# A mixture-of-experts stage with other weight rows, bfloat16 pair maps, and a branch and two down projections at other places

## The chip, the cores and the metric

The program runs on one core of one Trainium2 chip. The metric is device microseconds (us) from start to end of one execution, given as a median of runs. The engines of the core are named as in the profile: PE (TensorE, matrix products), PEld (its weight loads), DVE (VectorE), ACT (ScalarE), POOL (GpSimd) and SP (SyncE, which here only issues the transfers of weights).

## The reference, cut to what matters

Two transformer blocks work on 256 tokens of width 1024, in float32. The first one ends in a hierarchical mixture of experts: 4 groups of 4 experts, each token goes to 2 experts of one group, and each expert is a gated layer of width 512.

```python
def one_group(args):
    wg_g, wu_g, wd_g, comb_g = args
    hid = jax.nn.silu(jnp.einsum('td,edf->tef', t, wg_g)) * jnp.einsum('td,edf->tef', t, wu_g)
    return jnp.einsum('tef,efd->td', hid * comb_g[:, :, None], wd_g)

y = jnp.sum(lax.map(one_group, (wg, wu, wd, jnp.moveaxis(combine, 1, 0))), axis=0)
...
x = x + g2 * hierarchical_moe(hx2, ...)
return rmsnorm(x, final_norm_g)
```

The second block projects the result with `w_in_2` (10240 columns) and goes on with convolution, two kinds of attention and a dense layer of width 4096.

## The kernel before

One function issues everything by hand. Each engine runs its own instructions in the order in which they are written, and waits by semaphores for others. Weights come through one list, `plan`: SP loads the next entry (1 MB, with `kpn` as the layout) into one of 24 slots whenever `pump()` finds a free one, within the limits in `lim`. So loads run ahead of the work in a fixed order: per expert two halves of gate and up, then two halves of down, and after the last expert the pieces of `w_in_2`.

**Routing.** After attention, `xa_T` transposes x for the router's product, DVE ranks the logits, `posm` gets each token's slot (up to 64 tokens, `CAP`, in an expert) and `comb` its weight. `gather` builds the 64 columns of each expert in a group of four (`xg`) by a product with a 0/1 map (L1113).

**One expert e** (16 in a loop) is
- `moe_up(e, k0, k1)`, L1186: gate and up products side by side, two matmuls of 64 slots by 512 for each of eight slices of 128 rows; the trace counts each one twice,
- `moe_act(e)`, L1197 on ACT (silu) and L1198 on DVE (times up), result in `gm`,
- `moe_hT(e)`, L1204: four transposes of that result on PE; L1206 on DVE multiplies them by the slot weights `wb`,
- `moe_down(e)`, L1215: the down product, after which DVE (L1224, L1227) and ACT (L1225) scale it and split it in two parts (`RB`).

**One pair p of experts** has besides
- `weigh(p)`, L1151 and L1153 on DVE: the 0/1 map of tokens to slots, float32, and the map times `comb`,
- `slot_weights()`, L1160: a product with ones that lays the weights out by slot, copied to `wb` by L1161,
- `build_DT(p)`, L1168 and L1170: the map transposed in float32, one full and two half transposes for each half of the tokens, copied by ACT (L1172) to `DT`,
- `moe_comb(p)`, L1233: eight matmuls that add the pair's results into the four banks `yb`.

`weigh` stands at the end of an even expert; `slot_weights`, `build_DT` belong to the odd one behind it. In most experts a quarter or a half of `moe_up(e)` is written ahead of `moe_hT(e - 1)` and `moe_down(e - 1)`. A flag, `early`, turns this off:

```python
early = e >= 13 or (e and e % 4 == 0)
if not early:
    moe_up(e, 0, 2)
if e % 2:
    slot_weights()
if e:
    moe_hT(e - 1)
if not early:
    moe_up(e, 2, 4)
```

**The branch.** `beyond()` handles an expert with more than 64 tokens. Every engine loads the flag `over` (L1308) and branches (L1309); with these inputs the body is jumped over. It stands at the head of the last expert, e = 15, between `moe_comb(6)`, `weigh(7)` and `slot_weights`. The body uses PE, DVE, ACT and POOL.

Of the kernel before, what the change touches and what calls it, by code (L numbers as in the profile page):

```python
# [86 lines left out]
def body(tc, d, out, dbg=None, stop=None):  # L87
# [238 lines left out]
    def ld_x(t):  # L326
        nc.sync.dma_start(t, d["x"].rearrange("(t p) d -> p t d", p=128))
        nc.sync.dma_start(br, bass.AP(tensor=d["br"].tensor, offset=d["br"].offset, ap=[[0, 128], [1, 20]]))
        nc.sync.dma_start(wr, kpn(d["wr"]))

# [58 lines left out]
    for e in range(NE):  # L389
        for kh in range(2):  # L390
            for nm, w in (("g", d["w_gate"]), ("u", d["w_up"])):
                plan.append(((nm, e, kh), [128, 4, 512], kpn(w[e][512 * kh:512 * kh + 512, :])))
        for kh in range(2):
            plan.append((("d", e, kh), [128, 2, 1024], kpn(d["w_down"][e][256 * kh:256 * kh + 256, :])))
    w2 = d["w_in_2"]
# [207 lines left out]
    def mod_cols(Tn):  # L603
        bk = trans_bank([bm[:, Tn, j * 128:(j + 1) * 128] for j in range(4)])
        return bk.rearrange("p (j g r) -> p r g j", j=4, g=4)
# [538 lines left out]
    DT = None  # L1144
    wb = cp.tile([128, 2, 64], F32, name="wb")

    def map_of(i):
        return RA[:, 2, 256 * i:256 * i + 256].rearrange("p (t e c) -> p t e c", t=2, e=2)

    def weigh(p):  # L1150
        V.tensor_tensor(map_of(0), iot.to_broadcast([128, 2, 2, 64]),  # L1151
                        posm[:, :, 2 * p:2 * p + 2, None].to_broadcast([128, 2, 2, 64]), op=OP.is_equal)
        V.tensor_tensor(map_of(1), map_of(0),  # L1153
                        comb[:, :, 2 * p:2 * p + 2, None].to_broadcast([128, 2, 2, 64]), op=OP.mult)

    def slot_weights():

        bk = bank()
        for tt in range(2):
            T.matmul(bk[:, 0:128], ones, map_of(1)[:, tt].rearrange("p e c -> p (e c)"), start=(tt == 0), stop=(tt == 1))  # L1160
        V.tensor_copy(wb.rearrange("p e c -> p (e c)"), bk[:, 0:128])  # L1161

    def build_DT(p):

        bk = bank()
        Dp = map_of(0)
        for tt in range(2):
            T.transpose(bk[:, tt * 128:(tt + 1) * 128], Dp[:, tt].rearrange("p e c -> p (e c)"), ident)  # L1168
            for s in range(2):
                T.matmul(bk[64 * s:64 * s + 64, (2 + tt) * 128:(3 + tt) * 128], Dp[:, tt, 1 - s, :], ident,  # L1170
                         start=True, stop=True, skip_group_check=True)
        A.activation(DT, bk, AF.Copy)  # L1172
# [36 lines left out]
    def moe_down(e):  # L1209
        b = bank()  # L1210
        t = hTm.pop(e)
        for k in range(4):
# [4 lines left out]
            if k % 2:  # L1217
                raw_done(("d", e, k // 2))
        pump()
        pd = [(slice(64 * j, 64 * j + 64), j ^ (e % 2)) for j in range(2)]  # L1220
        if e == NE - 1:
# [85 lines left out]
    def beyond():  # L1307
        flag = nc.values_load(over[0:1, 0:1], min_val=0, max_val=1)  # L1308
        with tc.If(flag > 0):  # L1309
# [5 lines left out]
            h2T = take([128, 8, 256], F32, "h2b")  # L1315
            for k0, bk in transposed_pairs(lambda tt, k: xb[:, tt, k * 128:(k + 1) * 128], 8):
                for kk in range(2):
# [3 lines left out]
            hbT = take([128, 4, 256], F32, "hbT")  # L1321
            tmpD = take([128, 2, 512], F32, "tmpD")
            for e in range(NE):
                wt = {}
                for nm, w in (("g", d["w_gate"]), ("u", d["w_up"])):
                    for kh in range(2):
                        wt[nm, kh] = take([128, 4, 512], F32, "fb")
                        G.dma_start(wt[nm, kh], kpn(w[e][512 * kh:512 * kh + 512, :]))
                for tt in range(2):
# [10 lines left out]
                for dh in range(2):  # L1340
                    G.dma_start(wd[dh], kpn(d["w_down"][e][:, 512 * dh:512 * dh + 512]))
                for k0, bk in transposed_pairs(lambda tt, k: hb[:, tt, k * 128:(k + 1) * 128], 4):
                    V.tensor_copy(hbT[:, k0:k0 + 2], bk)
                for tt in range(2):
                    for dh in range(2):
                        bk = bank()
                        for k in range(4):
                            T.matmul(bk, hbT[:, k, tt * 128:(tt + 1) * 128], wd[dh][:, k, :], start=(k == 0), stop=(k == 3))
                        V.tensor_tensor(tmpD[:, dh], bk, gm[:, dh], op=OP.mult)
                        V.tensor_tensor(yb[tt][dh], yb[tt][dh], tmpD[:, dh], op=OP.add)  # L1350
                give(*wd)
            give(hb, hbT, tmpD, h2T)
        A.preload_act_table_set("silu_and_others")

    for e in range(NE):
        if e == NE - 3:
            lim[:] = [12, 4]
        if e == NE - 1:
            beyond()
        if e == 0:  # L1360
# [18 lines left out]
        if e == 1:  # L1379
# [31 lines left out]
        if e == 12:  # L1411
# [380 lines left out]
```

## Time and profile before

| | us |
|---|---|
| median of 3 runs | 1113.88 (1113.6 to 1114.24) |
| the profiled execution's own time | 1112.18 |
| its span, first to last instruction | 1110.4 |
| PE busy | 1057.2 (95%) |
| DVE busy | 606.0 (55%) |
| ACT busy | 434.3 (39%) |

The profiled execution lies 1.78 us above its span and 1.70 us under the median. The mean granted clock of PE is 0.987 of full speed. Busy shares are means over stages with different limits, so a stage is read from its own rows: in a timeline row the first two numbers are start and length, and brackets give the idle time before it and what ended that. The experts run from 318 to 559.5 us, the second block follows.

### The profile page before, as it was taken

What the parts mean: (1) busy time and instruction counts of PE and PEld (TensorE: products, weight loads), DVE (VectorE), ACT (ScalarE), POOL (GpSimd) and SP (SyncE); (2) the same over time, 40 slices, a digit from 0 to 9 for tenths busy, and PEclk for the clock granted to TensorE, in tenths of its full rate; (3) what the DMA queues carried; (4) which work ended last, traced back from release to release, by engine and by line L of the source; (5) the groups of instructions that cost most, each with busy time, mean ns of one, the idle gap of its engine ahead of it and who ended that gap; (6) DMA issues with size and microseconds to landing.
All of it is one profiled execution on the core that took longest, in us unless ns stands there. A gap on an engine that the chain in (4) does not pass through costs nothing.

```text
span 1110.4 us, 15119 instructions
## 1 busy us (share of the span) xinstructions
PE 1057.2 (95%) x6115; PEld 789.3 (71%) x6115; DVE 606.0 (55%) x930; ACT 434.3 (39%) x744; POOL 93.3 (8%) x99
## 2 busy tenths in 40 slices
PE   5999999899989999998689999999999999999998
PEld 4678876555743434343279878999888889998997
DVE  4554435666534343433175655767455676666544
ACT  4754213556312222222163476444435125343222
POOL 0000303000101010100010444000000000000000
PEclk9999999999989999999899999999999999999999
DMA  9979852454868999999913342534757565545611
GB/s 337 405 259 400 278 181 73 176 190 162 326 230 315 393 395 392 394 395 394 387 61 115 114 153 76 190 124 155 258 184 251 204 207 172 190 154 189 225 41 38
DMA packets 111087, 254.95 MB, mean 230 GB/s; under 512 B 5434, under 2 KB 8475, under 8 KB 108451
## 3 DMA queue, kind: packets, MB, share of 16 engines
q1 hardware_dynamic: 109666, 249.20, 62.4%
q0 software_dynamic: 1344, 4.72, 1.4%
q8 instruction: 50, 0.82, 0.3%
q14 instruction: 27, 0.21, 0.1%
HBM read 249.71 MB, written 4.19 MB: 229 GB/s over the span
## 4 chain that ended last, share of the span: by engine, by line
PE 48%; DMA 1%; DVE 1%; ACT 1%; SPq 0%; issue 0%; DVEq 0%; ACTq 0%
PE acc L223 26%; PE acc L243 11%; PE b L243 7%; DMA raw<-in_w_in 1%; PE b L483 1%; PE b L1499 1%; PE b L1521 1%; PE b L1577 1%; PE b L1601 1%; PE b L1215 0%; PE b L1532 0%; SPq L138 0%; PE b L1520 0%; DVE split L198 0%; ACT junkB L476 0%
## 5 line engine op out<-in xcount | busy, mean ns | idle before, releaser
L198 DVE TENSOR_TENSOR split<-raw,split 128x1024 fp32r<-128x1024 f32 (+2 forms) x226 | 267.5, 1212 | 79.5 <-ACT split L197 77.4
L197 ACT ACTIVATE split<-raw 128x1024 fp32r<-128x1024 f32 (+2 forms) x170 | 168.2, 1035 | 42.4 <-PE acc L223 14.5
L243 PE MATMUL acc<-uh,split 128*128 128x256 f32 x640 | 122.9, 288 | 1.4 <-ACT uh L498 1.4
L1186 PE MATMUL b<-raw,xg 128*64 128x512 f32 x512 | 115.8, 595 | 0.0
L243 PEld LDWEIGHTS acc<-uh,split 128*128 128x128 f32 x640 | 102.7, 193 | 2.5 <-ACT uh L498 1.6
L223 PE MATMUL acc<-split,uh 128*128 128x512 f32 x320 | 101.2, 392 | 0.0
L243 PE MATMUL b<-fh,split 128*128 128x256 f32 x512 | 93.9, 283 | 0.3 <-DVE split L198 0.3
L243 PE MATMUL acc<-ul,split 128*128 128x256 f32 x320 | 91.4, 286 | 0.1
L223 PE MATMUL acc<-split,hidT 128*128 128x512 f32 x384 | 88.4, 389 | 0.0
L223 PEld LDWEIGHTS acc<-split,hidT 128*128 128x128 f32 x384 | 71.6, 188 | 14.6
L243 PEld LDWEIGHTS b<-fh,split 128*128 128x128 f32 x512 | 80.4, 192 | 0.8 <-DVE split L198 0.5
L1186 PEld LDWEIGHTS b<-raw,xg 128*64 128x64 f32 x512 | 36.5, 137 | 61.1 <-issue 59.0
L243 PE MATMUL b<-fl,split 128*128 128x256 f32 x256 | 72.4, 283 | 0.0
L223 PEld LDWEIGHTS acc<-split,uh 128*128 128x128 f32 x320 | 60.1, 188 | 12.8
L1225 ACT ACTIVATE RB<-RA 64x512 fp32r<-64x512 f32 x32 | 20.1, 628 | 121.8 <-DVE RA L1224 120.2
L1215 PE MATMUL b<-raw,RA 128*64 128x512 f32 x256 | 60.0, 611 | 5.3 <-ACT xg L1121 2.5
L243 PEld LDWEIGHTS acc<-ul,split 128*128 128x128 f32 x320 | 61.9, 193 | 0.7 <-DVE ul L499 0.6
L223 PE MATMUL acc<-split,ul 128*128 128x512 f32 x160 | 62.3, 390 | 0.0
L1224 DVE TENSOR_TENSOR RA<-b,gm 64x512 f32<-64x512 f32 x32 | 22.0, 689 | 71.9 <-PE b L1215 71.4
L243 PEld LDWEIGHTS b<-fl,split 128*128 128x128 f32 x256 | 49.1, 192 | 0.3
L1215 PEld LDWEIGHTS b<-raw,RA 128*64 128x64 f32 x256 | 19.0, 141 | 39.8 <-issue 34.4
L223 PE MATMUL acc<-split,memTh 128*128 128x512 f32 x128 | 44.0, 413 | 3.2 <-ACT split L197 1.7
(398 smaller groups left out, 1741.4 us busy)
## 6 DMA issues: line engine op xcount, KB each, us to landing
raw<-in_w_up SPq DMA_DIRECT2D x48, 1024.0 KB, 5.5
raw<-in_w_down SPq DMA_DIRECT2D x48, 1024.0 KB, 9.1
raw<-in_w_in SPq DMA_DIRECT2D x46, 1024.0 KB, 7.9
raw<-in_w_gate SPq DMA_DIRECT2D x32, 1024.0 KB, 14.8
raw<-in_w_mod SPq DMA_DIRECT2D x24, 1024.0 KB, 11.3
raw<-in_w_mem_kv SPq DMA_DIRECT2D x8, 1024.0 KB, 14.1
raw<-in_w_out SPq DMA_DIRECT2D x8, 1024.0 KB, 5.0
raw<-in_w_conv_out SPq DMA_DIRECT2D x4, 1024.0 KB, 4.9
```

Of the source, the lines that this page charges most:

```text
L197: A.activation(s[:, 0], src, AF.Copy)
L198: V.tensor_tensor(s[:, 1], src, s[:, 0].bitcast(F32), op=OP.subtract)
L223: T.matmul(job.accs[m], x(k + kk), s[:, w, kk, :], start=job.start and first and kk == 0 and j == 0, stop=job.stop and last and kk == kg - ...
L243: T.matmul(bk[:, o:o + 256], s[:, w, kk, 128 * b:128 * b + 128], x(k + kk), start=first and b % per == 0 and r == 0 and kk == 0 and j == 0 ...
L483: T.transpose(bk[0:m, i * 128:i * 128 + p], s, ident)
L1186: T.matmul(b[64 * j:64 * j + 64, :], lt, raw((nm, e, k // 4))[:, k % 4, :], start=(k == 0), stop=(k == 7), skip_group_check=True)
L1215: T.matmul(b[64 * j:64 * j + 64, :], t[:, k, :], raw(("d", e, k // 2))[:, k % 2, 512 * dh:512 * dh + 512], start=(k == 0), stop=(k == 3), ...
L1224: V.tensor_tensor(RA[r, dh, :], b[r, :], gm[r, dh], op=OP.mult)
L1225: A.activation(RB[r, 0, dh, :], RA[r, dh, :], AF.Copy)
L1499: T.matmul(zb[i + j][:, o:o + 256 - k0], skT[sl, p, k0:k0 + 128], sqT[sl, p, k0:256], start=(o == 0), stop=False, skip_group_check=True)
L1521: T.matmul(b[:, 0:384], negL, v, start=False, stop=(n == 1), skip_group_check=True)
L1577: T.matmul(b[:, 0:256], xqT[:, 2 * h + dt, tt * 128:(tt + 1) * 128], mkT[:, 2 * h + dt, :], start=(dt == 0), stop=(dt == 1))
```

## The change

**Rows of 8 KB.** For gate, up and down weights (and the router's) a partition now holds neighbouring rows (`runs`), not every 128th one (`kpn`): gate and up come in one run of 8 KB for a partition where there were four of 2 KB, down in one of 8 KB where there were two of 4 KB. For that, whatever meets these rows is reordered: `xa_T`, `mod_cols` and `moe_hT` transpose every fourth or second column, and `xn` and `xh` are written from every fourth column.

**Maps in bfloat16.** `weigh` writes the 0/1 map in bfloat16, with a third copy, so that `build_DT` is four full products with a bfloat16 identity. The weights are split in two float32r parts (`ch`, `cl`), and `slot_weights` is four float32r products. `weigh(p + 1)` is called right behind `build_DT(p)`, one expert earlier.

**Other places.** `early` holds only for e = 4, 8, 12. `beyond()` stands at the end of e = 14. `moe_comb(6)`, `moe_down(14)` and `build_DT(7)` go behind `beyond()`: the first into `moe_up(15)`, the others after it. The body of the branch adds its results straight into `yb` on PE, and ACT and POOL take over most of what DVE did there.

```diff
+    def runs(ap, r):
+
+        return ap.rearrange("(p r) n -> p (r n)", r=r)
...
-                plan.append(((nm, e, kh), [128, 4, 512], kpn(w[e][512 * kh:512 * kh + 512, :])))
+                plan.append(((nm, e, kh), [128, 4, 512],
+                             lambda t, s=w[e][512 * kh:512 * kh + 512, :]: nc.sync.dma_start(flat(t), runs(s, 4))))
...
-        for k0, bk in transposed_pairs(lambda tt, k: x[:, tt, 512 * c + k * 128:512 * c + (k + 1) * 128], 4):
+        for k0, bk in transposed_pairs(lambda tt, k: x[:, tt, 512 * c + k:512 * c + 512:4], 4):
...
     def weigh(p):
-        V.tensor_tensor(map_of(0), iot.to_broadcast([128, 2, 2, 64]),
+        Dp = pair_map()
+        V.tensor_tensor(Dp[:, :, 0:2], iot.to_broadcast([128, 2, 2, 64]),
                         posm[:, :, 2 * p:2 * p + 2, None].to_broadcast([128, 2, 2, 64]), op=OP.is_equal)
-        V.tensor_tensor(map_of(1), map_of(0),
-                        comb[:, :, 2 * p:2 * p + 2, None].to_broadcast([128, 2, 2, 64]), op=OP.mult)
+        V.tensor_copy(Dp[:, :, 2], Dp[:, :, 0])
+        for w in range(2):
+            V.tensor_tensor(Dw[w].rearrange("p t (e c) -> p t e c", e=2), Dp[:, :, 0:2],
+                            combw[w][:, :, 2 * p:2 * p + 2, None].to_broadcast([128, 2, 2, 64]), op=OP.mult)
...
-        for tt in range(2):
-            T.matmul(bk[:, 0:128], ones, map_of(1)[:, tt].rearrange("p e c -> p (e c)"), start=(tt == 0), stop=(tt == 1))
+        for i in range(4):
+            T.matmul(bk[:, 0:128], onesr, Dw[i // 2][:, i % 2], start=(i == 0), stop=(i == 3))
...
-            T.transpose(bk[:, 64 * k:64 * k + 64], hd[:, k * 128:(k + 1) * 128], cst[64:128, C_ID + 64:C_ID + 128])
+            T.transpose(bk[:, 64 * k:64 * k + 64], hd[:, 256 * (k // 2) + k % 2:256 * (k // 2) + 256:2],
+                        cst[64:128, C_ID + 64:C_ID + 128])
...
-        early = e >= 13 or (e and e % 4 == 0)
+        early = e and e % 4 == 0
...
         if e:
             moe_hT(e - 1)
+        if e == NE - 1:
+            moe_comb(e // 2 - 1)
...
-        if e:
+        if e and e < NE - 1:
             moe_down(e - 1)
-        if e % 2:
+        if e % 2 and e < NE - 1:
             build_DT(e // 2)
+            weigh(e // 2 + 1)
...
-            weigh(e // 2)
+            if e == 0:
+                weigh(0)
+        if e == NE - 2:
+            beyond()
...
+    b14 = moe_down(NE - 2, False)
+    build_DT(NE // 2 - 1)
     moe_hT(NE - 1)
+    moe_out(NE - 2, b14)
     moe_down(NE - 1)
```

On PE, the rows around the branch stand so in the kernel before (L1233 is `moe_comb(6)`, L1160 `slot_weights`, L1204 `moe_hT(14)`, L1215 `moe_down(14)`, L1168 and L1170 `build_DT(7)`); the body, between the third and the fourth row, is left out:

```order
L1233 MATMUL acc_2551<-RB_2697,DT 128x512 x2
L1308 TENSOR_LOAD over
L1309 COMPARE_AND_BRANCH
...
L1309 UNCONDITIONAL_BRANCH x2
L1160 MATMUL b_5228<-RA_2654,ones 128x128 x2
L1204 MATMUL b_5232<-cst,gm_2690 128x64 x4
L1215 MATMUL b_5238<-raw_3527,RA_2654 64x512 x4
L1215 MATMUL b_5238<-raw_3544,RA_2654 64x512 x4
L1168 MATMUL b_5257<-cst,RA_2654 128x128
L1170 MATMUL b_5257<-cst,RA_2654 64x128 x2
```

And so in the changed one, whose L1215 is `moe_up`, L1189 `slot_weights`, L1233 `moe_hT(14)` and L1268 `moe_comb(6)`:

```order
L1215 MATMUL b_3673<-raw_3550,xg_3505 64x512
L1343 TENSOR_LOAD over
L1344 COMPARE_AND_BRANCH
...
L1344 UNCONDITIONAL_BRANCH x2
L1215 MATMUL b_5084<-raw_3571,xg_3505 64x512
L1215 MATMUL b_5084<-raw_3588,xg_3505 64x512
...
L1189 MATMUL b_5089<-Dw_2644,onesr 128x128 x2
L1189 MATMUL b_5089<-Dw_2645,onesr 128x128 x2
L1233 MATMUL b_5095<-cst,gm_2703 128x64 x4
L1268 MATMUL acc_2489<-RB_2710,DT 128x512 x2
```

The first work behind the branch was a product that reads a map of DVE's; now it is the first quarter of `moe_up(15)`.

On DVE, the rows ahead of the branch are these before (L1206 scales `moe_hT(13)`, L1224 and L1227 finish `moe_down(13)`, L1198 is `moe_act(14)`, L1151 and L1153 are `weigh(7)`); the body that follows has 197 rows before and 37 after (on ACT 32 and 64):

```order
L1206 TENSOR_TENSOR RA_2654<-b_3646,wb 128x256
L1224 TENSOR_TENSOR RA_2654<-b_3652,gm_2690 64x512 x2
L1227 TENSOR_TENSOR RB_2697<-RA_2654,RB_2697 64x512 x2
L1198 TENSOR_TENSOR gm_2690<-b_3667,gm_2690 64x512
L1151 TENSOR_TENSOR RA_2654<-cst,posm 128x256
L1153 TENSOR_TENSOR RA_2654<-RA_2654,comb 128x256
L1308 TENSOR_LOAD over
```

In the changed kernel `weigh(7)` (L1178 to L1182) stands in e = 13, behind the rows of `moe_down(12)` and ahead of `moe_act(13)` (L1227):

```order
L1262 TENSOR_TENSOR RB_2710<-RA_2663,RB_2710 64x512 x2
L1178 TENSOR_TENSOR RA_2663<-cst,posm 128x2x128
L1180 COPY RA_2663<-RA_2663 128x2x64
L1182 TENSOR_TENSOR Dw_2644<-RA_2663,ch 128x256
L1182 TENSOR_TENSOR Dw_2645<-RA_2663,cl 128x256
L1227 TENSOR_TENSOR gm_2703<-b_3617,gm_2703 64x512
```

Two DVE instructions for a pair have become four, and they stand some 10 us of work earlier.

## Rows read from the trace of the kernel before

**Rows 1.** PE's waits in the expert stage: total us, times, longest us

```profile
PE b L1204 <- DVE gm L1198: 3.0, 2, 1.5
...
PE b L1160 <- DVE RA L1153: 1.7, 3, 0.7
PE b L1215 <- DVE RA L1206: 1.6, 3, 0.5
...
PE b L1215 <- issue: 1.2, 2, 0.6
```

**Rows 2.** Waits of PE's weight loads there, one that a transfer ended

```profile
PEld b L1186 <- DMA raw<-in_w_gate: 0.4, 1, 0.4
```

**Rows 3.** Transfers from 380 to 513 us: rate, and down issues with us to landing

```profile
GB/s 411 392 386 385 402 405 391 386 386 405 402 387 387 392 405 404 384 386 392 408 394 389 388 395 405 392 386 384 402 407 388 387 387 401 407 387 387 390 403 398
...
raw<-in_w_down SPq DMA_DIRECT2D x16, 1024.0 KB, 14.0
```

**Rows 4.** SP's timeline, the last expert's down weights

```profile
513.07 3.76 SPq L138 DMA_DIRECT2D raw<-in_w_down  x2
```

**Rows 5.** PE's timeline in one odd expert, e = 5

```profile
386.88 0.71 PE L1160 MATMUL b<-RA,ones 128*128 128x128 f32 x4
387.52 0.46 PE L1204 MATMUL b<-cst,gm 64*128 64x64 f32 x4
...
389.68 3.60 PE L1215 MATMUL b<-raw,RA 128*64 128x512 f32 x16
393.21 0.33 PE L1168 MATMUL b<-cst,RA 128*128 128x128 f32 x1
...
394.37 0.60 PE L1186 MATMUL b<-raw,xg 128*64 128x512 f32 x2
```

**Rows 6.** PE's timeline, two bfloat16 products of 128x128 in the second block

```profile
618.25 0.23 PE L1516 MATMUL b<-maskb,identb 128*128 128x128 bf16 x1
618.32 0.22 PE L1517 MATMUL b<-maskb,identb 128*128 128x128 bf16 x1
```

**Rows 7.** DVE's timeline at the end of e = 2, beside POOL's work

```profile
352.21 0.42 DVE L1151 TENSOR_TENSOR RA<-cst,posm 128x256 f32<-128x256 f32 x1
352.67 2.61 DVE L1153 TENSOR_TENSOR RA<-RA,comb 128x256 f32<-128x256 f32 x1
```

**Rows 8.** PE's timeline from the down product of e = 13 on

```profile
514.16 3.65 PE L1215 MATMUL b<-raw,RA 128*64 128x512 f32 x16 [0.52 <-DVE RA L1206]
517.65 7.04 PE L1186 MATMUL b<-raw,xg 128*64 128x512 f32 x32
524.61 2.12 PE L1233 MATMUL acc<-RB,DT 128*128 128x512 f32 x8
533.22 1.20 PE L1160 MATMUL b<-RA,ones 128*128 128x128 f32 x4 [6.48 <-DVEq L1309]
...
535.59 5.53 PE L1215 MATMUL b<-raw,RA 128*64 128x512 f32 x16 [0.56 <-issue]
...
556.88 0.49 PE L1233 MATMUL acc<-RB,DT 128*128 128x512 f32 x1 [1.51 <-ACT RB L1225]
557.60 1.89 PE L1233 MATMUL acc<-RB,DT 128*128 128x512 f32 x7 [0.23 <-DVE RB L1227]
```

**Rows 9.** The branch: shortest/median/longest ns, first and last start in us

```profile
L1309 PEldq COMPARE_BRANCH  x1: 6008/6008/6008, 522.5 to 522.5; - x1
L1309 ACTq COMPARE_BRANCH  x1: 50/50/50, 525.4 to 525.4; - x1
...
L1309 DVEq COMPARE_BRANCH  x1: 72/72/72, 527.2 to 527.2; - x1
...
L1309 DVEq EVENT_SEMAPHORE  x1: 21/21/21, 533.1 to 533.1; - x1
```

**Rows 10.** A stretch behind the branch: length, busy us by engine, granted clock, transfers

```profile
533.20:541.10 7.90, 7.32 (x25) 3.15 (x25) 0.72 (x2) 0.00 (x0) 0.00 (x0) 0.61 1.05 385
```

**Rows 11.** Weight loads of the transposes, 318 to 525 us: count, busy us, mean ns

```profile
L1204 PEld LDWEIGHTS b<-cst,gm 64*128 64x128 f32 x52 | 4.2, 138 | 5.9 <-DVE gm L1198 4.8
```

More of the change, by code (lines that the diff above doesn't have):

```diff
@@ L328, in ld_x @@
         nc.sync.dma_start(br, bass.AP(tensor=d["br"].tensor, offset=d["br"].offset, ap=[[0, 128], [1, 20]]))
-        nc.sync.dma_start(wr, kpn(d["wr"]))
+        for h in range(2):
+            nc.sync.dma_start(flat(wr[:, 4 * h:4 * h + 4]), runs(d["wr"][512 * h:512 * h + 512, :], 4))
     plan.append(("x", [128, 2, 1024], ld_x))
@@ L391, in body @@
             for nm, w in (("g", d["w_gate"]), ("u", d["w_up"])):
-                plan.append(((nm, e, kh), [128, 4, 512], kpn(w[e][512 * kh:512 * kh + 512, :])))
+                plan.append(((nm, e, kh), [128, 4, 512],
+                             lambda t, s=w[e][512 * kh:512 * kh + 512, :]: nc.sync.dma_start(flat(t), runs(s, 4))))
         for kh in range(2):
-            plan.append((("d", e, kh), [128, 2, 1024], kpn(d["w_down"][e][256 * kh:256 * kh + 256, :])))
+            plan.append((("d", e, kh), [128, 2, 1024],
+                         lambda t, s=d["w_down"][e][256 * kh:256 * kh + 256, :]: nc.sync.dma_start(flat(t), runs(s, 2))))
     w2 = d["w_in_2"]
@@ L445, in body @@
     V.tensor_scalar(negL, Um, -1.0, None, op0=OP.add)
+    onesr = cp.tile([128, 128], F32R, name="onesr")
+    V.tensor_scalar(onesr, Um, 0.0, 1.0, op0=OP.mult, op1=OP.add)
     negO = cp.tile([128, 128], F32R, name="negO")
@@ L603, in mod_cols @@
     def mod_cols(Tn):
-        bk = trans_bank([bm[:, Tn, j * 128:(j + 1) * 128] for j in range(4)])
+        bk = trans_bank([bm[:, Tn, j::4] if Tn else bm[:, Tn, j * 128:(j + 1) * 128] for j in range(4)])
         return bk.rearrange("p (j g r) -> p r g j", j=4, g=4)
@@ L1028, in body, with fo, fi @@
     keep(1)
-    V.tensor_scalar(xn[:, 0, :], x[:, 0, :], r2[:, 0:1], None, op0=OP.mult)
+    def fo(t):
+        return t.rearrange("p (h j q) -> p h j q", h=2, j=4)
+    def fi(t):
+        return t.rearrange("p (h q j) -> p h j q", h=2, j=4)
+    V.tensor_scalar(fo(xn[:, 0, :]), fi(x[:, 0, :]), r2[:, 0:1], None, op0=OP.mult)
     for tt in range(2):
-        A.activation(xh[:, tt], x[:, tt, :], AF.Identity, scale=r2[:, tt:tt + 1])
-    A.activation(xn[:, 1, :], x[:, 1, :], AF.Identity, scale=r2[:, 1:2])
+        A.activation(fo(xh[:, tt]), fi(x[:, tt, :]), AF.Identity, scale=r2[:, tt:tt + 1])
+    A.activation(fo(xn[:, 1, :]), fi(x[:, 1, :]), AF.Identity, scale=r2[:, 1:2])
     for tt in range(2):
@@ L1133, in body @@
     V.tensor_tensor(comb, t16, c1[2][:, :, None].to_broadcast([128, 2, 16]), op=OP.mult)
+    ch, cl = smal([128, 2, 16], "ch", F32R), smal([128, 2, 16], "cl", F32R)
+    V.tensor_copy(ch, comb)
+    V.tensor_tensor(cl, comb, ch.bitcast(F32), op=OP.subtract)
+    combw = [ch.bitcast(F32), cl.bitcast(F32)]
     dump("comb", comb)
@@ L1145, in body, with pair_map @@
     wb = cp.tile([128, 2, 64], F32, name="wb")
-    def map_of(i):
-        return RA[:, 2, 256 * i:256 * i + 256].rearrange("p (t e c) -> p t e c", t=2, e=2)
+    Dw = [cp.tile([128, 2, 128], F32R, name=f"Dw{w}", tag=("cond", "rt")[w]) for w in range(2)]
+    def pair_map():
+        return RA[:, 2, 0:192].bitcast(BF).rearrange("p (t e c) -> p t e c", t=2, e=3)
     def weigh(p):
-        V.tensor_tensor(map_of(0), iot.to_broadcast([128, 2, 2, 64]),
+        Dp = pair_map()
+        V.tensor_tensor(Dp[:, :, 0:2], iot.to_broadcast([128, 2, 2, 64]),
                         posm[:, :, 2 * p:2 * p + 2, None].to_broadcast([128, 2, 2, 64]), op=OP.is_equal)
-        V.tensor_tensor(map_of(1), map_of(0),
-                        comb[:, :, 2 * p:2 * p + 2, None].to_broadcast([128, 2, 2, 64]), op=OP.mult)
+        V.tensor_copy(Dp[:, :, 2], Dp[:, :, 0])
+        for w in range(2):
+            V.tensor_tensor(Dw[w].rearrange("p t (e c) -> p t e c", e=2), Dp[:, :, 0:2],
+                            combw[w][:, :, 2 * p:2 * p + 2, None].to_broadcast([128, 2, 2, 64]), op=OP.mult)
     def slot_weights():
         bk = bank()
-        for tt in range(2):
-            T.matmul(bk[:, 0:128], ones, map_of(1)[:, tt].rearrange("p e c -> p (e c)"), start=(tt == 0), stop=(tt == 1))
+        for i in range(4):
+            T.matmul(bk[:, 0:128], onesr, Dw[i // 2][:, i % 2], start=(i == 0), stop=(i == 3))
         V.tensor_copy(wb.rearrange("p e c -> p (e c)"), bk[:, 0:128])
@@ L1165, in build_DT @@
         bk = bank()
[L1166 to L1171, printed above, removed]
+        Dp = pair_map()
+        for s in range(2):
+            for tt in range(2):
+                T.matmul(bk[:, (2 * s + tt) * 128:(2 * s + tt + 1) * 128],
+                         Dp[:, tt, s:s + 2].rearrange("p e c -> p (e c)"), identb,
+                         start=(s == 0 and tt == 0), stop=(s == 1 and tt == 1), skip_group_check=True)
         A.activation(DT, bk, AF.Copy)
@@ L1207, in moe_hT, with moe_down @@
                         op=OP.mult)
-    def moe_down(e):
+    def moe_down(e, evac=True):
         b = bank()
@@ L1219, in moe_down, with moe_out @@
         pump()
+        if evac:
+            moe_out(e, b)
+        return b
+    def moe_out(e, b):
         pd = [(slice(64 * j, 64 * j + 64), j ^ (e % 2)) for j in range(2)]
@@ L1315, in beyond @@
             h2T = take([128, 8, 256], F32, "h2b")
-            for k0, bk in transposed_pairs(lambda tt, k: xb[:, tt, k * 128:(k + 1) * 128], 8):
+            for k0, bk in transposed_pairs(lambda tt, k: xb[:, tt, 512 * (k // 4) + k % 4:512 * (k // 4) + 512:4], 8):
                 for kk in range(2):
@@ L1327, in beyond @@
                         wt[nm, kh] = take([128, 4, 512], F32, "fb")
-                        G.dma_start(wt[nm, kh], kpn(w[e][512 * kh:512 * kh + 512, :]))
+                        G.dma_start(flat(wt[nm, kh]), runs(w[e][512 * kh:512 * kh + 512, :], 4))
                 for tt in range(2):
@@ L1341, in beyond @@
                     G.dma_start(wd[dh], kpn(d["w_down"][e][:, 512 * dh:512 * dh + 512]))
+                    G.tensor_tensor(wd[dh], wd[dh], gm[:, dh:dh + 1].to_broadcast([128, 4, 512]), op=OP.mult)
                 for k0, bk in transposed_pairs(lambda tt, k: hb[:, tt, k * 128:(k + 1) * 128], 4):
-                    V.tensor_copy(hbT[:, k0:k0 + 2], bk)
+                    A.activation(hbT[:, k0:k0 + 2], bk, AF.Copy)
                 for tt in range(2):
                     for dh in range(2):
-                        bk = bank()
                         for k in range(4):
-                            T.matmul(bk, hbT[:, k, tt * 128:(tt + 1) * 128], wd[dh][:, k, :], start=(k == 0), stop=(k == 3))
-                        V.tensor_tensor(tmpD[:, dh], bk, gm[:, dh], op=OP.mult)
-                        V.tensor_tensor(yb[tt][dh], yb[tt][dh], tmpD[:, dh], op=OP.add)
+                            T.matmul(yb[tt][dh], hbT[:, k, tt * 128:(tt + 1) * 128], wd[dh][:, k, :], start=False,
+                                     stop=False, skip_group_check=True)
                 give(*wd)
-            give(hb, hbT, tmpD, h2T)
+            give(hb, hbT, h2T)
         A.preload_act_table_set("silu_and_others")
@@ L1357, in body @@
             lim[:] = [12, 4]
-        if e == NE - 1:
-            beyond()
         if e == 0:
@@ L1397, in body @@
         if e % 2 == 0:
-            if e:
+            if e and e < NE - 2:
                 moe_comb(e // 2 - 1)
-            weigh(e // 2)
+            if e == 0:
+                weigh(0)
+        if e == NE - 2:
+            beyond()
         if e % 4 == 2 and e < 12:
```

9 lines of the change are left out of this document (6 added, 3 removed).

## The prediction

> **What bounds the kernel now.** I first read the waits of PE between 318 and 560 us, the only stretch that the change touches on purpose. Busy shares there say that PE works nearly always; the list of waits says what stops it: DVE's map (L1160) and gate (L1204), DVE's scaling of hT (L1206) and two short unnamed stops, 7.5 us in all [rows 1], and besides them one stop of 6.48 us at the branch [rows 8]. Then I asked whether the weights are a second bound. The transfers run at about the same 385 to 410 GB/s throughout [rows 3], so the queue is full, yet PE's weight loads waited once, 0.4 us, for a transfer [rows 2]. The transfers run ahead of PE. So the experts are bound by PE, and each thing taken out of PE's own row counts in full until PE catches up with the transfers. The timelines of PE then give the lengths of the pieces.
>
> **8 KB rows: 0.** In rows 3 the rate alternates between some 387 GB/s (gate and up, runs of 2 KB) and some 404 (down, 4 KB), so longer runs do go faster: 1 MB takes 2.71 and 2.60 us. With 8 KB everything should take at most 2.60. But PE doesn't wait for them. The cover is their lead: the last down weights are issued at 513.07 and 14.0 us after issue they are there, 527 to 530 us [rows 3, 4]; `moe_down(15)`, which needs them, starts at 551.7, which is 16 us earlier by the sum below, 535. At the old rate the gate and up weights before them would be there by about 524.5, two transfers ahead; `moe_up(15)` would begin near 519 and come to its second half near 526. If the cover goes, at most 2 us are lost. Bounds 0 to +2, taken 0.
>
> **`build_DT`: -5.6.** Six float32 products stand between 393.21 and 394.37, 1.16 us [rows 5]. Four bfloat16 products replace them. Two such products of 128x128 in the second block start 0.07 us apart, 0.23 long [rows 6]: 3 x 0.07 + 0.15, about 0.36 us. 0.8 us in each of seven pairs (the eighth is in the tail below). Bounds for the new length: 0.28 (4 x 0.07) and 0.6 if each weight load shows; -6.2 to -3.9.
>
> **`slot_weights`: -1.0.** Now 386.88 to 387.52, 0.64 us for two float32 products, four passes in the trace [rows 5]. Four float32r products replace them. No product of this shape with float32r stands in these rows; between 4 x 0.07 and no gain at all, I take 0.5, so seven times -0.14 (-2.5 to 0).
>
> **`weigh`: waits -4.3, and +0.7 once.** Two DVE instructions of 0.42 us become four. Behind `build_DT(p)` they wait for PE's read of the old map; queued behind them is only `moe_act` of that expert, which must wait for 16 more matmuls anyway, 3.5 us, against 4 x 0.42. So the longer map is hidden, except for pair 0, which stays on the path in e = 0: two more instructions, +0.7. What the earlier place removes: at e = 2 the L1153 took 2.61 us beside POOL instead of 0.42 [rows 7], and the product of e = 3 waited for it; of the 1.7 us of L1160 I leave e = 1 its 0.6 and take 1.1. The stop of 0.6 in the same expert ("issue") goes with it. With `early` off for e = 13 and 14, a quarter of `moe_up` covers one of the two 1.5 us waits on `gm` and two of the three 0.5 us waits on L1206 [rows 1]: -1.5 and -1.05. Late next is hT's own chain, which a quarter of 1.76 us covers. Bounds -4.8 to -2.
>
> **The tail: -7.3.** From the end of `moe_up(14)`, 524.61, to the end of the last product, 557.60 + 1.89, it is 34.9 us [rows 8]. What stops PE there: PE's sequencer stays 6008 ns at its branch from 522.5, under cover of the queued work until 526.7; DVE branches at 527.2 in 72 ns, but its next event is at 533.1, 5.9 us later, and that is the one PE waits for. ACT shows 50 ns and nothing behind [rows 9]. The two long ones look like code that must be fetched.
>
> [...]
>
> DVE's body shrinks from 197 rows to 37, about the size at which ACT (32) did not stall; so I take DVE as free, and PE (still long) as 6.0. ACT's body grows from 32 to 64, nearer to 32 than to 197: free too.
>
> PE now reaches the branch after a quarter of `moe_up(14)`, `moe_down(13)` and half of `moe_up(14)`: 8 + 16 + 16 matmuls behind the last wait. Its sequencer took 8.3 us from 514.16 to 522.5 for 56 of them [rows 8, 9], 0.15 each, so 6.0 us for 40, and 6.0 at the branch: 12.0. The array needs 0.22 each (7.04 / 32), 8.8. Idle: 3.2 us instead of 6.5 (0 to 6.5). ACT and DVE have `moe_act(14)` ahead of their branch, up to 2 us after the array's end, inside the 3.2.
>
> After the stop of 6.48 the granted clock was 0.61 from 533.2 to 541.1 [rows 10], and `moe_down` took 5.53 instead of 3.60 [rows 5, 8]: 7.9 x 0.39 = 3.1 us lost. After a stop half as long no row says; 0 to 3.1, I take 2.0.
>
> So behind the end of `moe_up(14)`: idle 3.2, clock 2.0, `moe_up(15)` 7.0, `slot_weights` 0.5, hT 0.4, `moe_comb(6)` 2.1, `moe_down(14)` 3.5, `build_DT` 0.4, hT(15) 0.4 and its wait 0.5, `moe_down(15)` 3.5, the wait on the copies 1.5, `moe_comb(7)` with its small wait 2.6: 27.6 us, 7.3 less. The wait of hT(15) on `gm`, 1.5, goes since `moe_down(14)` now lies there.
>
> **Reads with a step: +1.0.** `xa_T` and hT read every fourth and second column. PE's load of hT's four columns is 138 ns, 52 times in the larger part of the stage [rows 11], 64 in all. If steps cost nothing it is 0; if they double each load it is 64 x 0.138 = 8.8, of which hT loads lie partly under other matmuls. Taken 1.0, near the lower end, because hT's matmuls are 0.1 apart at 0.46 for four, and its loads overlap them.
>
> [...]
>
> **Sum.** -5.6 - 1.0 + 0.7 - 4.3 - 7.3 + 1.0 + 0 = -16.5 us. The span 1110.4 becomes 1093.9 and the profiled execution 1112.18 becomes 1095.7; the median was 1.70 above that, so 1097.4.
>
> **The rivals.**
> - DVE or ACT still fetches code. For: DVE did, and 64 rows on ACT have no precedent. Against: ACT at 32. DVE's branch comes 8.8 + 1.7 us into that stretch and 5.9 are added: idle 7.6 instead of 3.2, the clock's 3.1 instead of 2.0: +5.5, 1103.
> - Steps cost more: two thirds of the 8.8 show, +5 to +6 in place of +1: 1102. For: hT is on PE's row in every expert. Against: loads overlap.
> - PE catches the transfers: a PE that is 9 us ahead by e = 15 has a margin of about 1.5 us on the gate and up weights. Up to +2: 1099. Against: longer rows go faster.
> - The slower side: the fetch at the branch lies behind the weights' packets. The transfers are full then (1.05 in rows 10), and packets of 8 KB are four times as long as those of 2 KB. If the fetch's 6.0 us is mostly such queueing, it becomes up to 24, and the gain of 16.5 is used up when it passes 22.5: 1115 at 24. Against: with runs of 2 and 4 KB mixed in the queues, PE and DVE stalled nearly alike, 6.0 and 5.9.
>
> **How the numbers follow.** My forecast (all terms near their values) 0.58; DVE or ACT fetches 0.14; steps 0.12; late weights 0.07; the long fetch 0.05; a gain beyond the sum (clock 0, idle 0, `build_DT` at 0.28: 5 to 6 us more) 0.04. Measurement tells this kernel from no change at about 0.2%, 2.2 us. All but the long fetch stay below 1111: faster 0.92, slower 0.05, the same 0.03, between them. The range: the likeliest case spans 1094 to 1101 by its own terms; 1091 takes in part of the clock and the idle at 0, 1106 the two rivals near 1103 with a term off beside them.
>
> **What would show each step.** In the profile after: `build_DT` as four products in about 0.36 us; no PE wait on a map from e = 3 on; hT(13) and hT(14) without a stop; DVE's event right after its branch; a PE idle near 3 us ahead of `moe_up(15)`; loads of hT at 138 ns; gate and up rates like those of down or better. The prediction is wrong if PE's branch takes far more than 6.0 us, if DVE's event is late again, if the hT loads double, or if PE's weight loads wait for transfers in e = 14 and 15.

## The result and the profile after

The changed kernel takes 1096.45 us (median of 4 runs, 1094.47 to 1097.79), the kernel before 1114.06 us; the ratio is 0.9844, with an interval of 0.983 to 0.9858. The forecast was 1097.4. The profiled execution took 1096.79 us; its span is 1095.0 us, 15.4 less than before.

First the waits of PE from 310 to 545 us (total us, times, longest us).

```profile
PE b L1215 <- PEq L1344: 2.6, 1, 2.6
...
PE b L1245 <- ACT xg L1141: 1.9, 3, 0.6
...
PE b L1189 <- DVE Dw L1182: 0.7, 1, 0.7
PE b L1245 <- ACT DT L1201: 0.6, 1, 0.6
```

What stood in [rows 1] is gone, but for the 0.7 us of expert 1. The waits on `xg` were 2.5 us before and are 1.9; the 0.6 us on `DT` are new. The stop at the branch is 2.6 us and now ends with PE's own sequencer (PEq), no longer with DVE's.

The timeline of PE in expert 5, to be held against [rows 5]:

```profile
382.49 0.66 PE L1189 MATMUL b<-Dw,onesr 128*128 128x128 f32 x4
383.08 0.69 PE L1233 MATMUL b<-cst,gm 64*128 64x64 f32 x4
383.70 1.94 PE L1215 MATMUL b<-raw,xg 128*64 128x512 f32 x8
...
389.00 0.40 PE L1198 MATMUL b<-identb,RA 128*128 128x128 bf16 x4
389.33 5.37 PE L1215 MATMUL b<-raw,xg 128*64 128x512 f32 x24
```

From start to start, `slot_weights` takes 0.59 us (0.64 before), `build_DT` 0.33 (1.16), and hT 0.62 (0.39): the one piece that became longer.

The branch (shortest/median/longest ns, first and last start in us), as [rows 9]:

```profile
L1344 PEldq COMPARE_BRANCH  x1: 5983/5983/5983, 511.1 to 511.1; - x1
...
L1344 DVEq COMPARE_BRANCH  x1: 72/72/72, 516.3 to 516.3; - x1
L1344 DVEq EVENT_SEMAPHORE  x1: 21/21/21, 516.9 to 516.9; - x1
L1344 PEldq EVENT_SEMAPHORE  x1: 51/51/51, 517.1 to 517.1; - x1
```

DVE's event follows 0.6 us after its branch, where it was 5.9. PE's branch is as long as before, 5.98.

The timeline of PE from the last down products on, as [rows 8], and the window behind the stop (columns as in [rows 10]):

```profile
511.33 3.60 PE L1215 MATMUL b<-raw,xg 128*64 128x512 f32 x16
517.49 2.44 PE L1215 MATMUL b<-raw,xg 128*64 128x512 f32 x8 [2.56 <-PEq L1344]
...
521.57 3.78 PE L1268 MATMUL acc<-RB,DT 128*128 128x512 f32 x8
525.28 5.52 PE L1215 MATMUL b<-raw,xg 128*64 128x512 f32 x24
...
541.62 2.48 PE L1268 MATMUL acc<-RB,DT 128*128 128x512 f32 x7 [0.23 <-DVE RB L1262]
```

```profile
517.49:525.30 7.81, 7.81 (x26) 4.52 (x26) 0.71 (x2) 0.00 (x0) 0.00 (x0) 0.58 1.05 385
```

The granted clock is 0.58 there, so `moe_comb(6)` takes 3.78 us where it took 2.12 [rows 8].

So the 15.4 us come from three stretches. The experts start at 316.21 instead of 318.26: 2.05. From there to the end of `moe_up(14)` (524.61 before, 511.33 + 3.60 = 514.93 after): 9.68 less 2.05, 7.63. From there to the end of the last `moe_comb` (34.88 us before, 544.10 - 514.93 = 29.17 after): 5.71. Behind it the two executions run alike.

The first stretch was not in the forecast, and it has two parts. From PE's last products ahead of the ranking (302.39 before, 302.50 after) to the first product of `gather` it is 9.31 us before and 8.40 after, 0.9 less; DVE's ranking fills most of that. `gather` itself, until the experts start, takes 6.56 before and 5.31 after:

```profile
311.70 2.05 PE L1113 MATMUL b<-D,xh 128*128 128x256 f32 x8 [1.10 <-DVE tot L1079]
...
315.25 1.91 PE L1113 MATMUL b<-D,xh 128*128 128x256 f32 x8
```

```profile
310.90 2.05 PE L1133 MATMUL b<-D,xh 128*128 128x256 f32 x8 [2.12 <-DVE tot L1099]
...
314.25 1.09 PE L1133 MATMUL b<-D,xh 128*128 128x256 f32 x8
```

These products are the same in number and shape in both kernels; the granted clock is 0.55 before and 0.71 after. In other profiles `gather` takes 5.45 us with the start of the kernel before (the run with the body alone) and 6.70 with that of the changed one (the run with down in 4 KB runs), so these 1.25 us go with the execution, not with the change. This is the timeline of DVE, ACT and POOL in the ranking of the experts, before and then after:

```profile
301.46 2.19 ACT L1031 ACTIVATE xh<-raw,r_r 128x1024 fp32r<-128x1024 f32 x2 [0.82 <-DVE r_r L472]
...
302.69 4.74 POOL L1034 TENSOR_TENSOR xlo<-xn,xh 128x1024 fp32r<-128x1024 f32 x2 [3.33 <-ACT xh L1031]
303.00 2.23 DVE L1048 TENSOR_TENSOR cmp<-lg 128x160 f32<-128x160 f32 x1
...
305.16 2.46 DVE L1049 TENSOR_TENSOR cmp<-lg 128x160 f32<-128x160 f32 x1
```

```profile
301.59 4.19 ACT L1051 ACTIVATE xh<-raw,r_r 128x1024 fp32r<-128x1024 f32 x2 [0.82 <-DVE r_r L486]
...
303.10 0.33 DVE L1068 TENSOR_TENSOR cmp<-lg 128x160 f32<-128x160 f32 x1
...
303.83 2.37 POOL L1054 TENSOR_TENSOR xlo<-xn,xh 128x1024 fp32r<-128x1024 f32 x1 [4.45 <-ACT xh L1051]
303.94 2.45 DVE L1072 TENSOR_TENSOR cmp<-cmp 128x160 f32<-128x160 f32 x1
...
307.87 2.34 POOL L1054 TENSOR_TENSOR xlo<-xn,xh 128x1024 fp32r<-128x1024 f32 x1 [1.66 <-ACT xn L1052]
...
309.04 1.72 DVE L1094 TENSOR_TENSOR D<-cst,posm 128x512 fp32r<-128x512 f32 x1
```

Beside a subtraction of POOL (`xlo`) a comparison of DVE lasts 2.2 to 2.5 us where it takes 0.33 otherwise, and `slots_of` (L1094) 1.72; the short `posm` at 308.82, 0.19 us as before, is not stretched. ACT now reads every fourth column and needs 4.19 us instead of 2.19 for the two `xh`; POOL, which waits for it, starts 1.1 us later and breaks in the middle, and DVE's chain meets it once in the ranking, not twice, and once more at `slots_of`. That is the 0.9 us.

### The profile page after: what moved, and what is told of

It is laid out like the page before. It is cut to its first block, busy times and chain, and to the rows that moved or that the text cites. A ratio compares the mean times of both kernels' runs of the same rounds, so it can differ in the third digit from the quotient of the medians.

```text
span 1095.0 us, 15061 instructions
## 1 busy us (share of the span) xinstructions
PE 1054.9 (96%) x6067; PEld 790.1 (72%) x6067; DVE 601.0 (55%) x949; ACT 437.2 (40%) x744; POOL 92.0 (8%) x99
## 3 DMA queue, kind: packets, MB, share of 16 engines
HBM read 249.71 MB, written 4.19 MB: 232 GB/s over the span
## 4 chain that ended last, share of the span: by engine, by line
PE 50%; DMA 1%; DVE 1%; ACT 1%; issue 0%; DVEq 0%; ACTq 0%
PE acc L232 26%; PE acc L252 11%; PE b L252 7%; DMA raw<-in_w_in 1%; PE b L497 1%; PE b L1215 1%; PE b L1539 1%; PE b L1561 1%; PE b L1617 1%; PE b L1641 1%; PE b L1572 0%; PE acc L1268 0%; PE b L1560 0%; DVE split L207 0%; ACT junkB L490 0%
## 5 line engine op out<-in xcount | busy, mean ns | idle before, releaser
L1215 PE MATMUL b<-raw,xg 128*64 128x512 f32 x512 | 117.7, 600 | 2.6 <-PEq L1344 2.6
L1215 PEld LDWEIGHTS b<-raw,xg 128*64 128x64 f32 x512 | 35.9, 137 | 64.2 <-issue 61.2
L1759 ACT ACTIVATE hid<-b 128x512 f32<-128x512 f32 x16 | 9.5, 596 | 91.3 <-PE b L252 91.3
```

The lines of the kernel that those rows point to most:

```text
L1215: T.matmul(b[64 * j:64 * j + 64, :], lt, raw((nm, e, k // 4))[:, k % 4, :], start=(k == 0), stop=(k == 7), skip_group_check=True)
```

## The experiments

Each is timed against runs of the kernel before on the same chip; three chips were used, with medians of before of 1114.53, 1113.36 and 1114.72 us. Ratios are those to the kernel before.

**Down in 4 KB runs.** Does the step of two in hT cost what the rows say?

```diff
-                         lambda t, s=d["w_down"][e][256 * kh:256 * kh + 256, :]: nc.sync.dma_start(flat(t), runs(s, 2))))
+            plan.append((("d", e, kh), [128, 2, 1024], kpn(d["w_down"][e][256 * kh:256 * kh + 256, :])))
-            T.transpose(..., hd[:, 256 * (k // 2) + k % 2:256 * (k // 2) + 256:2],
+            T.transpose(..., hd[:, k * 128:(k + 1) * 128],
```

> The changed kernel, but the down weights come in two runs of 4 KB again and moe_hT transposes neighbouring columns. Theory: the step of two is what makes each transpose group last 0.62 us instead of 0.39 and its loads 210 ns instead of 143; undone 16 times this gives back 16 x 0.23 = 3.7 us, and the slower transfers of down stay hidden: 1092.8. Rival: the transfers with 8 KB rows are what lets PE run earlier; then PE's weight loads wait for down weights in e = 13 to 15 and the time is 1096.5 or more.

Measured: 1093.72 us, ratio 0.9813 (0.9794 to 0.9832), 0.0031 or 3.5 us under the changed kernel; the two intervals just touch, so the rows have to decide. hT is back at 0.39 us from start to start. From the start of the experts to the end of `moe_up(14)` it is 196.2 us here and 198.7 in both profiles of the changed kernel, 2.5 less: 14 x 0.23 = 3.2, of which 0.6 go into longer waits on `xg` (2.5 instead of 1.9 us). The step is the cost, about 3 us of it net with the two hT in the tail. The groups of weight loads from 318 to 525 us, in the changed kernel and in this one (count, busy us, mean ns):

```profile
L1233 PEld LDWEIGHTS b<-cst,gm 64*128 64x128 f32 x56 | 7.7, 210 | 4.2 <-DVE gm L1227 3.2
```

```profile
L1232 PEld LDWEIGHTS b<-cst,gm 64*128 64x128 f32 x56 | 4.5, 138 | 4.1 <-DVE gm L1226 3.2
```

**No 8 KB rows.** As above, and gate, up and router weights by `kpn` too, with every read on neighbouring columns.

> The changed kernel with no 8 KB rows and no read with a step at all. Theory: hT gives back 3.7 us as in the kernel with down alone; the start of the experts goes back to where it was before (318.3 instead of 316.2 us), since POOL's two subtractions again lie beside DVE's ranking as before: +2.05; together 1094.8. Rival: with 2 KB rows PE, now some 16 us ahead, catches the transfers; PE's loads then wait for gate and up weights of e = 14 and 15, and it is 1097 or more.

Measured: 1096.37 us, 0.984 (0.9821 to 0.9859), some 3.0 us more than with down alone, where 2.05 was expected; the intervals just overlap. In its profile PE waits 4.8 us for `selm` and the experts start at 318.0, as before. By the rows only 0.9 us of that are POOL's: from PE's last products ahead of the ranking to `gather` it is 9.30 us, as before, where it is 8.42 with down alone. I had taken 2.05, which includes the clock in `gather`. The experts until the end of `moe_up(14)` take 196.2 us as there. The rest of the 3.0 us stands in no row that the edit changes. No matmul waits for a transfer. So the gate and up rows are worth something here only by the way they shift POOL, about 0.9 us.

**The subtractions on DVE.** This tests that, on the kernel with down in 4 KB runs.

```diff
-    for tt in range(2):
-        G.tensor_tensor(xlo[:, tt], xn[:, tt], xh[:, tt].bitcast(F32), op=OP.subtract)
...
+    V.tensor_tensor(xlo[:, 0], xn[:, 0], xh[:, 0].bitcast(F32), op=OP.subtract)
     start_y(1, 1)
...
     slots_of(0)
+    V.tensor_tensor(xlo[:, 1], xn[:, 1], xh[:, 1].bitcast(F32), op=OP.subtract)
```

> The kernel with down in 4 KB runs, and POOL's two subtractions (xlo) written on DVE, one behind selm, one behind the first slots_of. Theory: POOL's subtractions are what stretches a DVE comparison from 0.32 to 2.45 us and slots_of from 0.69 to 1.72; without them the experts start some 3 us earlier, 313 instead of 316.2: 1089.8. Rival: DVE's two additional instructions of 1.2 us lie on the path as long as what they free: 1092.8, no better than that kernel.

Measured: 1089.05 us, 0.9779 (0.9762 to 0.9796), another 3.8 us less by the ratios; its slowest run, 1090.67, lies under the fastest with POOL's subtractions, 1091.9. DVE's timeline:

```profile
303.98 0.32 DVE L1069 TENSOR_TENSOR cmp<-cmp 128x160 f32<-128x160 f32 x1
...
305.01 1.22 DVE L1076 TENSOR_TENSOR xlo<-xn,xh 128x1024 fp32r<-128x1024 f32 x1
...
306.36 0.69 DVE L1092 TENSOR_TENSOR D<-cst,posm 128x512 fp32r<-128x512 f32 x1
```

Without POOL the comparison takes 0.32 instead of 2.45 us and `slots_of` 0.69 instead of 1.72; from PE's last products ahead of the ranking to `gather` it is 4.65 us instead of 8.42, and the experts start at 312.58. By its median this is the fastest kernel of all, 2.2% under before where the changed one is 1.6% under.

**The same without any 8 KB row.**

> The kernel without any 8 KB row, with POOL's two subtractions on DVE as in the kernel that did the same with gate and up in 8 KB rows. Theory: the rows are worth nothing even with PE 20 us ahead of before: 1089, as that kernel. Rival: PE catches the transfers of 2 KB rows: its weight loads wait for them and it is 1092 or more.

Measured: 1090.72 us, 0.9783 (0.9769 to 0.9796): not to be told from the kernel above. But its profile shows the first wait of PE for a transfer:

```profile
513.25 3.21 PE L1204 MATMUL b<-raw,xg 128*64 128x512 f32 x6 [0.62 <-DMA raw<-in_w_up]
```

So with 2 KB rows PE has just caught up with the transfers, at the head of expert 15, for 0.6 us. The rows may begin to be worth something there; the times do not show it.

**The rows alone**, on the kernel before.

> The kernel before with the 8 KB rows and their reads with a step, and nothing else. Theory: the quicker transfers are worth nothing, hT costs 16 x 0.23 = +3.7, the start of the experts gains 2.05: 1115.7. Rival: the rows are part of the gain: 1112 or less.

Measured: 1114.5 us, 1.0005 (0.9993 to 1.0016). The theory's 1115.7 (1.0015) lies at the end of the interval, the rival's 1112 (0.998) outside. The profile has both parts, hT at 0.62 and the experts' start at 316.37, of which again 0.9 us is DVE's chain and the rest the clock in `gather`. The rows are no part of the gain. One row I had not looked for: PE's branch takes 3.43 us here, over the old body, which takes 6.0 in the kernel before. Why is open; the stop, 5.85 us, still ends with DVE.

**The body alone**, on the kernel before, its branch at the old place.

> The kernel before with the changed body of the branch alone (short on DVE), the branch at its old place. Theory: DVE's stall of 5.9 us behind the branch is a fetch that its long body causes; with the short one its event comes within 1 us, and PE waits only for its own 6.0 us, until 528.6: idle 1.9 instead of 6.5 us, and between 0 and 3.1 us of clock come back: 1106.4 to 1109.5. Rival: the length of the body has nothing to do with it, 1114.

Measured: 1110.2 us, 0.9965 (0.9952 to 0.9978), 3.9 us less by the ratio. Its branch and the stop behind it:

```profile
L1309 PEldq COMPARE_BRANCH  x1: 6087/6087/6087, 524.2 to 524.2; - x1
...
L1309 DVEq COMPARE_BRANCH  x1: 72/72/72, 528.9 to 528.9; - x1
L1309 DVEq EVENT_SEMAPHORE  x1: 21/21/21, 529.5 to 529.5; - x1
```

```profile
530.65 0.68 PE L1160 MATMUL b<-RA,ones 128*128 128x128 f32 x4 [2.22 <-PEq L1309]
```

DVE's event is on time, and the stop is 2.2 instead of 6.5 us: the old body made DVE late. That it is the number of its rows, 197 or 37, and not something else in them, is argued. The median's gain is about the stop's 4.3. In this profile the clock gave nothing back: behind the stop `moe_down(14)` takes 6.42 us (5.53 before), and `moe_down(13)`, ahead of it, 5.33 (3.65 before).

**The old body at the new place.**

> The changed kernel with the old body of the branch (long on DVE), the branch at its new place. Theory: DVE's event comes 5.9 us after its branch again, at 522.3; PE's idle is 7.4 instead of 2.6 us, the clock loses up to 0.4 us more: 1101.3 to 1101.7. Rival: the new place hides it: 1096.5.

Measured: 1101.64 us, 0.9898 (0.9883 to 0.9914), 6.0 us more than the changed kernel by the ratios. The stop:

```profile
523.66 3.68 PE L1215 MATMUL b<-raw,xg 128*64 128x512 f32 x8 [7.33 <-DVEq L1344]
```

The rival that DVE is still late is so priced: it would have cost 4.8 us by the stop and 6.0 by the times.

**One expert in the body**, `for e in range(1)` in `beyond`.

> The changed kernel with a body of the branch that handles one expert instead of sixteen (it leaves out fifteen experts of the overflow, which these inputs don't need), so that PE's body is short too. Theory: PE's branch falls from 5.98 us to under 0.1, but PE then waits for DVE, whose branch stands behind the gate of expert 14: the stop shrinks from 2.6 to 2.0 us, 1096. Rival: PE's own branch is all there is to the stop: it falls below 0.5 us, 1094 or less.

Measured: 1097.73 us, 0.9839 (0.9823 to 0.9854): no change. The branch and the stop:

```profile
L1344 PEldq COMPARE_BRANCH  x1: 1905/1905/1905, 511.4 to 511.4; - x1
...
L1344 DVEq EVENT_SEMAPHORE  x1: 21/21/21, 517.2 to 517.2; - x1
```

```profile
517.47 1.94 PE L1215 MATMUL b<-raw,xg 128*64 128x512 f32 x8 [2.25 <-DVEq L1344]
```

PE's branch shrinks to 1.9 us, not under 0.1, but the stop stays at 2.25, now with DVE's event as its end: DVE branches only at 516.6, behind the gate of expert 14. Two waits of nearly the same length lie over each other, and a shorter body on PE moves next to nothing here.

**No branch.** `beyond()` is not called; only ACT's table load at its end stays.

> The changed kernel without the branch (it leaves out the handling of experts with more than 64 tokens, which these inputs don't need). Theory: the stop of 2.6 us and the 2.7 us that the lower clock costs from 517.5 to 526 both go: 1091.2. Rival: the clock falls for another reason, only the stop goes: 1093.9.

Measured: 1093.26 us, 0.9812 (0.9797 to 0.9828), 3.6 us less by the ratios, between the two. In its profile both stop and low clock are missing at this place (`moe_comb(6)` takes 2.13 us). Why the median gains less than 5.3, the next run bears on. Besides, this profile reaches the experts only at 319.64 us, 3.4 later than the changed kernel's, with a granted clock of 0.97 and 0.93 in 150 to 200 and 200 to 250 us where that one has 1.00 and 0.97, in work that no edit here touches.

**The changed kernel again.**

> The changed kernel once more, unaltered, for a second profile. Theory: the clock behind a stop of one and the same length differs between executions, so the stop is 2.6 us again and the time lost to the clock behind it is not 2.7 us again, but anything from 0 to 3; median 1094.5 to 1098. Rival: the loss belongs to the stop and is 2.7 us again.

Measured: 1096.72 us, 0.9837 (0.9823 to 0.9851). The same stop in this second profile, and the window behind it:

```profile
517.78 1.94 PE L1215 MATMUL b<-raw,xg 128*64 128x512 f32 x8 [2.56 <-PEq L1344]
...
520.86 2.11 PE L1268 MATMUL acc<-RB,DT 128*128 128x512 f32 x8
```

```profile
517.78:525.60 7.82, 7.82 (x38) 4.03 (x40) 0.72 (x2) 0.00 (x0) 0.00 (x0) 1.00 1.05 385
```

The stop is the same to 0.01 us, and the clock is 1.00 instead of 0.58. Its span is 1092.8, 2.2 less. So what one profile shows of the clock behind a stop is no property of the stop; in these two executions it is worth 0 and 2.7 us, and 3.6 - 2.6 = 1.0 us is what the runs without the branch give for it on the average, uncertain by more than that.

**Old places.** Branch, `early`, `moe_comb(6)`, `moe_down(14)` and `build_DT(7)` where they were; rows, maps and body new.

> The changed kernel with the branch, the last comb, down and map products and the flag early at their old places; rows, maps and body are the new ones. Theory: the waits of hT(13), moe_down(12) and moe_down(13) come back (+2.5), the wait of hT(15) on the gate and its scaling (+1.5), the idle at the branch is 1.9 instead of 2.6 (-0.7): 1099.8, or 1097 if a stop of 1.9 us leaves the clock alone. Rival: the places are most of the gain in the tail: 1102 or more.

Measured: 1105.34 us, 0.9913 (0.9893 to 0.9933), 7.7 us more than the changed kernel by the ratios. My theory said 3.3; the rival, from 1102 on, was right. PE's timeline:

```profile
510.07 5.16 PE L1245 MATMUL b<-raw,RA 128*64 128x512 f32 x16 [0.52 <-DVE RA L1236]
...
526.58 0.90 PE L1189 MATMUL b<-Dw,onesr 128*128 128x128 f32 x4 [2.45 <-PEq L1344]
...
528.66 6.09 PE L1245 MATMUL b<-raw,RA 128*64 128x512 f32 x16 [0.52 <-DVE RA L1236]
```

The waits come to 4.4 us more than in the changed kernel, not 3.3: 3.0 on the gate and 2.1 on the scaling of hT, less 0.6 on `DT` and 0.1 at the branch. And `moe_down` takes 5.16 and 6.09 instead of 3.65: 4 us more, which I take for a low clock, behind stops of 1.5, 0.5 and 2.45 us in this execution. That every run of this kernel has them isn't shown; its runs reach from 1100.25 to 1106.47. Behind the same stops of 1.5 and 0.5 us, `moe_down(13)` takes 3.65 us in the profile of before, 5.35 with the rows alone and 5.33 with the body alone. So the places are worth the 4.4 us of waits; the other 3.3 of the 7.7 go with the clock in the main, and how many of them belong to the places one profile can't tell.

**Maps in float32**, early as in the changed kernel.

> The changed kernel with the maps, slot_weights and build_DT of before in float32; the early call of weigh, the rows and the places are the new ones. Theory: build_DT takes 1.16 instead of 0.33 us in eight pairs and slot_weights 0.05 more: +7.0, 1103.5. Rival: the gain came from weigh's earlier place, the form of the products is worth less: 1099 or less.

Measured: 1104.2 us, 0.9905 (0.9887 to 0.9922), 7.6 us more than the second series of the changed kernel on the same chip. From the start of the experts to the end of `moe_up(14)` the profile takes 204.3 us where both profiles of the changed kernel take 198.7: 5.6 of the 7.6 us stand there, and the eighth pair's 0.8 in the tail. The form of the products is a gain by itself, whatever the place of `weigh`. The place keeps its own part here: of the 1.7 us that PE waited for the map [rows 1], 0.6 are left. No run takes the place back alone.

## Why the prediction was right, by its steps

**The sum**, -16.5 to the span, became -15.4, and it was right partly because errors met. Too favourable by 3.9 us were the reads with a step (1.6 ahead of the tail), the tail (1.6) and `slot_weights` (0.7). Against them stood 2.9 us that came out better: the start of the experts, 2.05, which was not in the sum and of which 1.25 are the clock in `gather` in these two executions, then `weigh` (0.6) and `build_DT` (0.2). The step to the median was luck too: I added 1.70, as before, but here the median lies 0.34 under the profiled execution. So the profiled execution was forecast 1.1 us too low (1095.7 for 1096.79) and the median 0.95 too high.

**`build_DT`**: forecast -5.6, measured 7 x 0.83 = -5.8, and the experiment with float32 maps agrees. **`slot_weights`**: -1.0 forecast, 7 x 0.05 = -0.35 measured; four products in float32r are hardly shorter than two in float32. **`weigh`**: the +0.7 in expert 0 was +0.1, since the longer map was nearly hidden there; the waits removed were -4.3 as forecast, 1.7 of them by the early place and 2.5 by `early`, as the rows show; no run takes either back alone.

**Reads with a step** is the term that was mis-sized: taken +1.0, it was 16 x 0.23 = 3.7 for hT, 3.1 after the 0.6 us that the waits on `xg` became shorter. I argued from loads that overlap their matmuls; the rows show that four loads of 210 instead of 138 ns each, 0.29 us in all, lengthen the group by 0.23: most of it stands bare. The rival "steps cost more" had the mechanism right, at somewhat less than its +5 to +6. With a step PE's loads take 210 ns (two, hT) and 212 (median; four, `xa_T`) in the changed kernel, against 138 and 140 without one in the kernel before: the step of two is as dear as the step of four. ACT's two `xh`, with a step of four, take 4.19 us instead of 2.19.

**8 KB rows**: 0 forecast, and the kernel with the rows alone is at 1.0005. They move more bytes: some 420 GB/s in the slices of the experts (the fifteenth on; the span is cut in 40) where [rows 3] has some 387 to 404, but no matmul waits, and none did before. The weight loads of the kernel before waited three times, not once: beside [rows 2] the same view has two waits of 0.3 us on `in_w_up`. The changed kernel's first profile has no such wait.

```profile
GB/s 354 404 244 403 272 179 90 173 212 141 310 258 328 403 422 420 421 420 414 363 1 155 116 116 100 171 154 193 231 184 264 200 197 163 184 177 186 215 39 39
```

**The tail**: -7.3 forecast, -5.7 measured. Idle 2.56 (3.2 forecast): PE's sequencer reached the branch sooner than 0.15 us for each matmul allowed. The clock cost 2.7 us (2.0), and 0.6 more at the last `moe_comb`, which I had at full speed; two hT of 0.23 more make 0.5. These are 1.1 of the 1.6 us; the rest are pieces rounded down by 0.1 or so. The 2.7 were near the 2.0 by luck: the second profile has none of them. DVE's and ACT's new bodies did not stall, as taken, and the runs with the old body and with the new one alone show that DVE's body decides it.

That the long stops are fetches of code was my estimate from their lengths; no run shows it. What the runs show is 6.0 us for PE, 5.9 for DVE with the long body, 0.6 for DVE with the short one and 1.9 for PE with one expert. DVE's branch itself takes 72 ns with either body, and only the event behind it is late. The lists of DMA queues name two queues "instruction", with packets of 16 KB (q8, 50 in the whole execution) and most of 8 KB (q14, 27). In the kernel before, a packet of q8 is listed at 526.0 us, inside PE's branch (522.5 to 528.5), one of q14 at 531.0 and one of q8 at 531.75, in the stretch in which DVE is late (527.2 to 533.1). In the changed kernel one of q8 is listed at 514.5 us, inside PE's branch (511.1 to 517.1), and none of either queue in the 0.6 us from DVE's branch to its event. Which engine a queue serves the trace does not say, and what makes PE's branch 1.9 us with one expert and 3.43 with the rows alone stays open. The rival of the long fetch, a stop of up to 24 us behind 8 KB packets, fell: PE's branch takes 5.98 us with them, 6.01 without.

## What to carry to other kernels

Longer runs of bytes were worth nothing here (1.0005 with the rows alone) while PE did not wait for a transfer; the reads with a step that they forced on others cost at once (hT 0.62 us instead of 0.39), so look first whether such a read is hidden. A branch jumped over kept PE 6.0 us and DVE 5.9 here, and 1.9 and 0.6 with a shorter body; shorten the one that is late, and look which wait ends second before shortening further. Compare variants over several executions, and stretch by stretch, when the clock falls in one of them: 2.7 us of one profile here belonged to no edit.

## What the hardware showed that I had not expected

The granted clock behind one and the same stop of 2.56 us was 0.58 in one execution and 1.00 in another. A step of two floats in PE's weight loads costs as much as a step of four, half as much again as none (210 and 212 ns, against 138 and 140). PE's branch over a body of sixteen experts took 3.43 us with the rows alone, and 5.98 to 6.20 in the kernel before, the changed one and the runs with the body alone and with the old body. And a comparison of DVE that takes 0.32 us lasts 2.2 to 2.5 beside a subtraction of POOL, so that making ACT slower, and POOL later, brought the experts forward by 0.9 us.
